# A transformer layer in fp32r parts on one Trainium2 core: whole blocks of the up product 512 columns wide, steps around the transposes and the down product's forms reordered, and the down weights of the second pass moved to another place modulo 256 bytes

## The chip, the cores and the metric

The kernel runs on one core of a Trainium2 chip. The metric is the time of one execution on the device in microseconds (us), taken several times, with the median as the figure to compare. One further execution is recorded by the hardware profiler; its timeline is called the trace here. The engines are named as the profile names them: PE (TensorE, matmuls) with PEld (its weight loads), DVE (VectorE), ACT (ScalarE), POOL (GpSimd) and SP (SyncE, which issues most of the DMAs).

## The reference

One layer over a sequence of 512 rows, width 1024, in float32:

```python
h  = _rmsnorm(x, g_pre_mix)
...
merged = jax.nn.sigmoid(a_ret) * y_ret + jax.nn.sigmoid(a_sgu) * y_sgu
x = x + _rmsnorm(merged @ w_out, g_post_mix)
h2 = _rmsnorm(x, g_pre_ffn)
x = x + _rmsnorm(_conv_gated_mlp(h2, w_up, conv_w, conv_b, w_down), g_post_ffn)
```

`y_ret` is a bidirectional retention (four heads, chunks of 128 rows), `y_sgu` a spatial gating unit. `_conv_gated_mlp` multiplies h2 by w_up (1024 x 5632, the *up product*), runs a depthwise convolution of three taps along the sequence, takes gelu of the first half times the second (2816 columns), and multiplies by w_down (2816 x 1024, the *down product*). `merged @ w_out` is called the *output product* below. The change touches the stretch from the output product to the end.

## The kernel before

**Parts.** A float32 product is made of three matmuls of fp32r operands. Each operand is split into a high and a low part (`split`, lines 85 to 87): ACT copies the high part (L80), DVE subtracts it from the source and so writes the low part (L87). `mm3` (lines 218 to 221, the matmuls' rows L219 to L221) issues high by high, high by low and low by high. In a matmul the first operand is the stationary one (128 x 128, loaded ahead by PEld), the second the moving one; the number of moving columns, 256 (*narrow*) or 512 (*wide*), is the matmul's length. Sums lie in PSUM banks of 512 columns; a bank is free again when DVE or ACT has read it.

**Weights.** They lie in DRAM as 146 units of 128 x 1024, in the order of use, and SP loads each by one DMA into one of 4 `raw` buffers. `w_get` hands out the next unit and makes the splits of up to four units ahead, so the splits' place on ACT and DVE follows the order of the program: what the program issues ahead of a `w_get` stands ahead of that unit's splits in their queues. The parts go to nine slots of 1088 floats (4352 bytes, 17 x 256). The second argument of `slot` (L124) is an offset in floats. In the built program a slot without an offset begins at 64 bytes modulo 256; with 16 floats it begins at 128, with 48 at 0. This *place* modulo 256 bytes is meant when the text says that a part lies at 0, 64 or 128. The other tiles of 512 floats (`blk`) begin at 64.

**Up product.** It has 44 blocks of 128 columns of w_up: 22 tiles in the gated half and as many in the other. Two kinds of steps make them. Tiles that are not in a couple are *whole blocks* (`up_block` L933, `h2_block` L927): weights stationary, the parts of h2 transposed (h2h, h2l) moving, first for the rows 0 to 255 (`T0`), then for 256 to 511 (`T1`), 24 narrow matmuls each. Sixteen tiles form eight couples: the two blocks of the first are made by a 2 x 2 scheme of the Strassen kind with seven products of 12 narrow matmuls instead of eight (`Pair`, L660, matmuls at L676), whose weight sums DVE and POOL make (L166 to L170, `wf` are their parts), and the two of the second are whole blocks, between the parts of the first. `c` tiles collect a Pair's results (L704 is one such reading of a bank). The output gate products earlier in the kernel (`gated_pair`) have the same scheme, with whole blocks that are 512 wide already (`f_block`, L646).

**Turns.** After the output product of a tile of 128 rows, `norms` (L858) makes x1 and scales it (L882); `turn` (L890) transposes it on PE, with ACT copying the high parts and raw copies, and DVE making the low parts (L901). Tiles 0 and 1 are turned during the output products of tiles 2 and 3. Then four blocks (`EARLY`) of the up product run on T0, with the turn of tile 2 behind the first of them and the turn of tile 3 behind the fourth, and then the same four on T1. `row_scale` takes a power on POOL (L849).

**Down product.** It has two passes, one for each half of the output columns. A pass has nine steps (`products`, L1050, matmuls at L1062), each with the seven products of the 2 x 2 scheme over a pair of gated tiles, 42 narrow matmuls, and four tiles outside the scheme (`add_whole`, L1068, matmuls at L1079). Here the activations are stationary and the weights (`q` and `t` units, parts dh and dl) move. A step's activation side is made by `down_forms` (L994): five DVE steps of 256 columns and three of 512, with their copies on ACT. Seven of the nine *forms* (`EAGER`) are made while the up product runs, the last two ahead of the second and the fourth step of the first pass, and the four tiles outside the scheme are split ahead of its first four steps. At the end of a pass DVE and ACT read the banks and add them up (`steps`; L1094 is the second sum of `after7`), which frees the banks for the second pass. Then rows are scaled, added to x1 and written.

Of the kernel before, what the change touches and what calls it, by code (L numbers as in the profile page):

```python
# [10 lines left out]
F32 = mybir.dt.float32  # L11
# [17 lines left out]
LOOK = 4  # L29
NBLK = 76  # L30
WARM = 18
# [3 lines left out]
WHOLE = NF - 2 * DP  # L35
EAGER = 7
ADDED = (0, 2)
# [11 lines left out]
def tile_block(ctx: ExitStack, tc, xT, x, wall, par, cs, wsp, bsp, gpost, gpre, gffn, out):  # L49
# [11 lines left out]
    def blk(dt=F32, n="blk", shape=(P, S)):  # L61
        return sb.tile(list(shape), dt, tag="blk", bufs=NBLK, name=nm(n))

    def tmp(n="tmp", shape=(P, S)):
        return sb.tile(list(shape), F32, tag="tmp", bufs=6, name=nm(n))
# [19 lines left out]
    def split(hi, lo, src):  # L85
        copy(hi, src)
        nc.vector.tensor_sub(lo, src, as32(hi))  # L87

# [7 lines left out]
    while i < NW:  # L96
# [19 lines left out]
        else:  # L116
            units.append(("blk", i))
            i += 1
    w_ready, w_pos, w_held, w_raw = {}, [0, 0], [0], {}

# [6 lines left out]
    def w_block(i):  # L127
# [48 lines left out]
    def w_down(form, i):  # L176
# [61 lines left out]

    xh, xl, xg = [], [], {}

    def load_x(k):
        t = tmp("xT")
        nc.sync.dma_start(t, xT[k])
        h_, l_ = blk(F32R, "xh"), blk(F32R, "xl")
# [598 lines left out]
    def row_scale(q):  # L843
# [9 lines left out]
    gpm, gpf = bcast(gpost, "gpm"), bcast(gpre, "gpr")  # L853
    h2h, h2l, h2r = ([[blk(dt, n) for _ in range(4)] for _ in range(2)]
                     for dt, n in ((F32R, "h2h"), (F32R, "h2l"), (F32, "h2r")))
    x1 = [[dp_.tile([P, S], F32, tag=f"x1_{t}{n}", name=f"x1_{t}{n}") for n in range(2)] for t in range(NT)]

    def norms(t, acc):  # L858
# [9 lines left out]
        for n in range(2):  # L868
            z = tmp("z")
            v.scalar_tensor_tensor(  # L870
                out=z, in0=acc[n], scalar=sc, in1=gpm[n], op0=ALU.mult, op1=ALU.mult
            )
            v.tensor_add(xt[n], xt[n], z)
            mean_square(q, n, xt[n])
            nc.gpsimd.dma_start(x1[t][n], xt[n])
            if n == 0 and t in ADDED:
                nc.gpsimd.dma_start(out[t, :, 0:S], xt[0])
        sc, _ = row_scale(q)
        zs = []
# [7 lines left out]

    two = "p (i n) -> p i n"

    def turn(t, zs):  # L890
        g, c = t // 2, slice((t % 2) * P, (t % 2 + 1) * P)
        for n in range(2):
            p = ps()
            for f in range(4):
                nc.tensor.transpose(p[:, f * P : (f + 1) * P], zs[n][:, f * P : (f + 1) * P], ident)
            for i in range(2):
                hi, lo, raw = (h[g][2 * n + i].rearrange(two, i=2)[:, :, c] for h in (h2h, h2l, h2r))
                pf = p[:, 2 * i * P : 2 * (i + 1) * P].rearrange(two, i=2)
                copy(hi, pf)
                copy(raw, pf)  # L900
                v.tensor_sub(lo, pf, as32(hi))  # L901

    def h2(k, t):
        f = slice((k % 2) * 256, (k % 2 + 1) * 256)
        g = t.start // 256
        return h2h[g][k // 2][:, f], h2l[g][k // 2][:, f]

# [18 lines left out]

    def h2_block(w, o, q):  # L927
# [12 lines left out]

    early_w, early_o = [], []

    def early(e, q):

        if q == 0:
            early_w.append(w_get(1))
            early_o.append(ps())
        h2_block(early_w[e], early_o[e], (T0, T1)[q])

    dn_ = Down(mh, ml, KD, RES_OUT)  # L950
    zs = {}
    for t in range(NT):
        acc = [dn_.finish(t, 0)]
        if t > 1:
            turn(t - 2, zs[t - 2])
        acc.append(dn_.finish(t, 1))
        zs[t] = norms(t, acc)
    early(0, 0)
    turn(2, zs[2])
    for e in range(1, EARLY):  # L960
        early(e, 0)
    turn(3, zs[3])
    for e in range(EARLY):
# [24 lines left out]

    def two_parts(t):
        h_, l_ = blk(F32R, "fh"), blk(F32R, "fl")  # L990
        split(h_, l_, t)
        return h_, l_

    def down_forms(j):  # L994
# [8 lines left out]
        v.tensor_add(a[:, T1], b[:, T0], s_[:, T1])  # L1003
        bh, bl = two_parts(b)
        sh, sl = two_parts(s_)
        th, tl = two_parts(a)
        dforms.append({
# [99 lines left out]
    for j in range(DP):  # L1107
        if j < WHOLE:
            whole.append(two_parts(gp[2 * DP + j]))
        if j % 2 and late:  # L1110
            down_forms(late.pop(0))
        products(m, j, steps if j == DP - 1 else {})
        if j in (3, 5):
            w = w_get()
# [209 lines left out]
```

## Time and profile before

| | |
|---|---|
| time, median of 3 runs | 829.57 us (828.09 to 830.15) |
| the profiled execution's own time | 826.92 us |
| its span | 825.1 us |
| PE busy | 814.5 us (99% of the span) |
| DVE, ACT, POOL busy | 658.5, 429.7, 104.2 us |
| output product, with the turns of tiles 0 and 1 | 426.3 to 471.6 us |
| four early blocks, with the turns of tiles 2 and 3 | 471.6 to 518.4 us |
| other blocks of the up product | 518.4 to 703.9 us |
| down product, first and second pass | 703.9 to 760.5, 760.5 to 816.4 us |

The stretches are read from the first matmul of each. "Busy" of PE counts a matmul from its start to a modelled end, and the ends of pipelined matmuls overlap; so the interval between the starts of two matmuls tells what one costs. The page names instructions by line, engine, operation, and `out<-in` with the program's tile names; a shape as 128x512 is partitions by elements. Where the profile names a releaser, it is the work on another engine whose end let the instruction start.

### The profile page before, as it was taken

What the parts mean: (1) busy time and instruction counts of PE and PEld (TensorE: products, weight loads), DVE (VectorE), ACT (ScalarE), POOL (GpSimd) and SP (SyncE); (2) the same over time, 40 slices, a digit from 0 to 9 for tenths busy, and PEclk for the clock granted to TensorE, in tenths of its full rate; (3) what the DMA queues carried; (4) which work ended last, traced back from release to release, by engine and by line L of the source; (5) the groups of instructions that cost most, each with busy time, mean ns of one, the idle gap of its engine ahead of it and who ended that gap; (6) DMA issues with size and microseconds to landing.
All of it is one profiled execution on the core that took longest, in us unless ns stands there. A gap on an engine that the chain in (4) does not pass through costs nothing. (4 is left out here: it accounts for less than half of the span.)

```text
span 825.1 us, 14353 instructions
## 1 busy us (share of the span) xinstructions
PE 814.5 (99%) x5728; PEld 756.6 (92%) x5728; DVE 658.5 (80%) x1076; ACT 429.7 (52%) x733; POOL 104.2 (13%) x108
## 2 busy tenths in 40 slices
PE   9999999999999999999999999999999999999995
PEld 7888888888999999999988899999999999999995
DVE  7489897878898687767765579679899899997956
ACT  6636445536665444444444556456566566644532
POOL 0010000103221111132221201111111100000002
PEclk9999999999999999999999999999999999999999
DMA  8733222213233333233459111333333341243334
GB/s 284 256 116 102 77 77 77 77 52 94 74 105 127 103 103 101 80 101 102 123 173 355 64 54 50 104 102 103 103 103 103 102 155 52 77 141 104 114 129 128
DMA packets 29252, 93.84 MB, mean 114 GB/s; under 512 B 3392, under 2 KB 4032, under 8 KB 29184
## 3 DMA queue, kind: packets, MB, share of 16 engines
q1 hardware_dynamic: 26784, 86.58, 32.5%
q0 software_dynamic: 1968, 6.03, 2.4%
q8 instruction: 45, 0.74, 0.4%
q10 hardware_dynamic: 432, 0.30, 0.1%
q14 instruction: 23, 0.19, 0.1%
HBM read 88.19 MB, written 4.72 MB: 113 GB/s over the span
## 5 line engine op out<-in xcount | busy, mean ns | idle before, releaser
L87 DVE TENSOR_TENSOR wl<-raw,wh 128x1024 fp32r<-128x1024 f32 (+1 forms) x93 | 109.6, 1187 | 49.2 <-PE ps L676 26.5
L80 ACT ACTIVATE wf<-raw 128x512 fp32r<-128x512 f32 x140 | 85.0, 626 | 102.4 <-PE ps L220 42.7
L87 DVE TENSOR_TENSOR wf<-raw,wf 128x512 fp32r<-128x512 f32 x140 | 110.1, 801 | 26.1 <-ACT wf L80 25.4
L220 PE MATMUL ps<-h2l,wh 128*128 128x256 f32 x448 | 123.7, 277 | 0.2 <-DVE h2l L901 0.2
L219 PE MATMUL ps<-h2h,wh 128*128 128x256 f32 x448 | 123.3, 277 | 0.0
L221 PE MATMUL ps<-h2h,wl 128*128 128x256 f32 x448 | 123.3, 276 | 0.0
L676 PE MATMUL ps<-sh,wf 128*128 128x256 f32 x640 | 119.1, 277 | 0.1
L80 ACT ACTIVATE wh<-raw 128x1024 fp32r<-128x1024 f32 (+2 forms) x95 | 93.0, 989 | 35.5 <-DMA raw<-wall 14.0
L676 PEld LDWEIGHTS ps<-sh,wf 128*128 128x128 f32 x640 | 100.7, 188 | 0.8 <-DVE c L704 0.3
L676 PE MATMUL ps<-sl,wf 128*128 128x256 f32 x320 | 88.5, 277 | 0.0
L220 PEld LDWEIGHTS ps<-h2l,wh 128*128 128x128 f32 x448 | 84.0, 188 | 0.7 <-DVE h2l L901 0.7
L219 PEld LDWEIGHTS ps<-h2h,wh 128*128 128x128 f32 x448 | 83.8, 188 | 0.3 <-ACT h2h L80 0.3
L221 PEld LDWEIGHTS ps<-h2h,wl 128*128 128x128 f32 x448 | 83.9, 188 | 0.0
L481 PE MATMUL ps<-wh,xh 128*128 128x512 f32 x192 | 75.0, 391 | 0.0
L482 PE MATMUL ps<-wl,xh 128*128 128x512 f32 x192 | 74.9, 390 | 0.0
L483 PE MATMUL ps<-wh,xl 128*128 128x512 f32 x192 | 74.8, 390 | 0.0
L168 POOL TENSOR_TENSOR raw<-raw,raw 128x512 f32<-128x512 f32 x20 | 34.9, 1743 | 241.0 <-DVE raw L166 217.0
L1062 PE MATMUL ps<-dh,fl 128*128 128x256 f32 x216 | 61.0, 282 | 0.0
L1062 PE MATMUL ps<-dl,fh 128*128 128x256 f32 x216 | 60.3, 279 | 0.5 <-DVE dl L87 0.5
L1062 PE MATMUL ps<-dh,fh 128*128 128x256 f32 x216 | 60.6, 280 | 0.0
L676 PEld LDWEIGHTS ps<-sl,wf 128*128 128x128 f32 x320 | 60.1, 188 | 0.5 <-issue 0.2
L676 PE MATMUL ps<-xh,wf 128*128 128x256 f32 x288 | 53.6, 278 | 0.0
(309 smaller groups left out, 2035.0 us busy)
## 6 DMA issues: line engine op xcount, KB each, us to landing
raw<-wall SPq DMA_DIRECT2D x145, 512.0 KB, 3.6
x<-x SPq DMA_DIRECT2D x22, 256.0 KB, 5.7
xT<-xT SPq DMA_DIRECT2D x8, 256.0 KB, 5.3
x<-x POOLq DMA_DIRECT2D x8, 256.0 KB, 2.4
xT<-xT POOLq DMA_DIRECT2D x4, 256.0 KB, 4.3
out<-zs SPq DMA_DIRECT2D x3, 256.0 KB, 3.4
cs<-cs SPq DMA_DIRECT2D x2, 256.0 KB, 4.0
gpm<-gpost POOLq DMA_DIRECT2D x2, 256.0 KB, 3.7
```

What stands on the lines that cost most here:

```text
L80: nc.scalar.activation(out=o, in_=i, func=AF.Copy)
L87: nc.vector.tensor_sub(lo, src, as32(hi))
L168: nc.gpsimd.tensor_tensor(out=w_raw["T2"], in0=w_raw["T1"], in1=w_raw["B22"], op=ALU.add)
L219: nc.tensor.matmul(o, ah, bh, start=start, stop=False)
L220: nc.tensor.matmul(o, ah, bl, start=False, stop=False)
L221: nc.tensor.matmul(o, al, bh, start=False, stop=stop)
L481: nc.tensor.matmul(acc[t], xh[k][:, c], wh[:, f], start=k == 0, stop=False)
L482: nc.tensor.matmul(acc[t], xh[k][:, c], wl[:, f], start=False, stop=False)
L483: nc.tensor.matmul(acc[t], xl[k][:, c], wh[:, f], start=False, stop=k == KD - 1)
L676: nc.tensor.matmul(o, w_[:, c], a_, start=first and k == n == 0, stop=k == 3 and n == 2, skip_group_check=True,)
L1062: nc.tensor.matmul(o, a_[:, c], w_[:, f], start=j == t == i == 0, stop=j == DP - 1 and i == 2 and n not in (M2, M3, M4), skip_group_check= ...
```

## The change

- **Width.** The whole blocks of the up product behind the four early ones, 24 of them, run all 512 rows in one matmul: 24 wide ones for each block instead of 48 narrow ones. So that a matmul can take 512 rows at once, h2h and h2l lie in tiles of twice the width (`two`), with all rows of one 128-wide piece of the width side by side. `Pair.part3`, which ran between the two halves of a block, now runs in its middle. Weight slots of these blocks have no offset any more. The early blocks stay in halves.
- **Turns.** In `turn` the high copies and the low parts come first, the raw copies last. The scaling is taken out of `norms` into `scaled`, and that of tile 2 is issued behind the low parts of the turn of tile 1. The turn of tile 3 comes in the middle of the fourth early block.
- **Late forms.** `EAGER` is 5 instead of 7. The four later forms and the four tiles outside the scheme are issued behind the steps of the first pass, from a list, and each group is placed behind the low part of the next step's `t` weights (`tc.issue_after`).
- **Places in the down product.** In the first pass both weight parts of a step keep their offsets; in the second both have 48, so all moving parts lie at 0 there; the stationary ones stay at 64.

```diff
-            hi, lo = (slot("wh", 16), slot("wl", 48)) if i >= DOWN0 else (
-                (slot("wh", 48), slot("wl", 16)) if i >= UP0 else (slot("wh"), slot("wl"))
+            hi, lo = (slot("wh", 48), slot("wl", 48)) if i >= DOWN0 + DP + WHOLE // 2 else (
+                (slot("wh", 16), slot("wl", 48)) if i >= DOWN0 else
+                (slot("wh", 48), slot("wl", 16)) if UP0 <= i < UP0 + EARLY else (slot("wh"), slot("wl"))
             )
...
-        hi, lo = slot("dh", 16, w), slot("dl", 48, w)
-        split(hi, lo, raw)
+        at = (16, 48) if i < DOWN0 + DP + WHOLE // 2 else (48, 48)
+        hi, lo = slot("dh", at[0], w), slot("dl", at[1], w)
+        w_low[form, i] = split(hi, lo, raw).ins
...
             for i in range(2):
-                hi, lo, raw = (h[g][2 * n + i].rearrange(two, i=2)[:, :, c] for h in (h2h, h2l, h2r))
...
                 copy(hi, pf)
-                copy(raw, pf)
-                v.tensor_sub(lo, pf, as32(hi))
+                low = v.tensor_sub(lo, pf, as32(hi))
+                raws.append((raw, pf))
+        for raw, pf in raws:
+            copy(raw, pf)
+        return low
...
     def up_block(between=None):
-        w, o = w_get(), ps()
-        h2_block(w, o, T0)
-        if between:
-            between()
-        h2_block(w, o, T1)
+        (wh, wl), o = w_get(), ps()
+        for k in range(KD):
+            if between and k == KD // 2:
+                between()
+            c = slice(k * P, (k + 1) * P)
+            mm3(o, wh[:, c], wl[:, c], *h2(k, slice(0, S)), k == 0, k == KD - 1)
         return o
...
         acc = [dn_.finish(t, 0)]
         if t > 1:
-            turn(t - 2, zs[t - 2])
+            low = turn(t - 2, zs[t - 2])
+        if t == 3:
+            with tc.issue_after(low.ins):
+                zs[2] = scaled(*xq)
         acc.append(dn_.finish(t, 1))
-        zs[t] = norms(t, acc)
+        xq = norms(t, acc)
+        if t != 2:
+            zs[t] = scaled(*xq)
     early(0, 0)
     turn(2, zs[2])
     for e in range(1, EARLY):
-        early(e, 0)
-    turn(3, zs[3])
+        early(e, 0, (lambda: turn(3, zs[3])) if e == EARLY - 1 else None)
...
-    late = list(range(EAGER, DP))
+    later = (("w", 0), ("w", 1), ("f", 5), ("w", 2), ("f", 6), ("w", 3), ("f", 7), ("f", 8))
...
     for j in range(DP):
-        if j < WHOLE:
-            whole.append(two_parts(gp[2 * DP + j]))
-        if j % 2 and late:
-            down_forms(late.pop(0))
         products(m, j, steps if j == DP - 1 else {})
+        if j + 1 < DP:
+            with tc.issue_after(w_low["t", DOWN0 + j + 1]):
+                for kind, i in {0: later[:1], 1: later[1:3], 2: later[3:4], 3: later[4:6], 4: later[6:7], 5: later[7:]}.get(j, ()):
...
```

The program has 5115 matmuls and transposes afterwards instead of 5691. Besides those rows on PE, the order moves at three places on DVE. Line numbers afterwards are a little higher for the same statement: L87 is L91, L901 is L911, L882 is L893, L704 is L712.

The first place is DVE during the output product of the last tile of rows, where the turn of tile 1 is read: `h2l` are the low parts of h2, `xn` the scaled tile 2, `x` its x1. Before:

```order
L873 TENSOR_TENSOR x_844_4735<-x_844_4735,z_4755 128x512
L846 SCALAR_TENSOR_TENSOR qs_4761<-q_4747 128x1
L882 SCALAR_TENSOR_TENSOR xn_4765<-x_843_4734,qr_4762,gpr_4379 128x512
L882 SCALAR_TENSOR_TENSOR xn_4767<-x_844_4735,qr_4762,gpr_4380 128x512
L901 TENSOR_TENSOR h2l_4391<-ps_4787,h2h_4383 128x2x128
L901 TENSOR_TENSOR h2l_4393<-ps_4798,h2h_4385 128x2x128
L901 TENSOR_TENSOR h2l_4392<-ps_4787,h2h_4384 128x2x128
L901 TENSOR_TENSOR h2l_4394<-ps_4798,h2h_4386 128x2x128
```

And now:

```order
L881 TENSOR_TENSOR x_828_4719<-x_828_4719,z_4739 128x512
L911 TENSOR_TENSOR h2l_4379<-ps_4763,h2h_4375 128x2x128
L911 TENSOR_TENSOR h2l_4380<-ps_4763,h2h_4376 128x2x128
L911 TENSOR_TENSOR h2l_4381<-ps_4772,h2h_4377 128x2x128
L911 TENSOR_TENSOR h2l_4382<-ps_4772,h2h_4378 128x2x128
L854 SCALAR_TENSOR_TENSOR qs_4785<-q_4731 128x1
L893 SCALAR_TENSOR_TENSOR xn_4789<-x_827_4718,qr_4786,gpr_4371 128x512
L893 SCALAR_TENSOR_TENSOR xn_4791<-x_828_4719,qr_4786,gpr_4372 128x512
```

The four low parts stand ahead of the two scaling steps (and the step in front of those) instead of behind them.

The second place is DVE in a couple of the up product, where a weight sum for the next couple is made: `raw` are the sums, `wf` their parts, `fl` a part of a form, `c` a Pair's result, whose reading frees a bank. Before:

```order
L87 TENSOR_TENSOR fl_6507<-gp_5314,fh_6506 128x512
L166 TENSOR_TENSOR raw_6585<-raw_6562 128x512
L167 TENSOR_TENSOR raw_6562<-raw_6562,raw_6563 128x512
L87 TENSOR_TENSOR wf_6589<-raw_6585,wf_6589 128x512
L704 TENSOR_TENSOR c_6511<-ps_6514,c_6511 128x256
L87 TENSOR_TENSOR wf_6641<-raw_6585,wf_6641 128x512
```

And now:

```order
L91 TENSOR_TENSOR fl_6203<-gp_5250,fh_6202 128x512
L171 TENSOR_TENSOR raw_6281<-raw_6258 128x512
L172 TENSOR_TENSOR raw_6258<-raw_6258,raw_6259 128x512
L712 TENSOR_TENSOR c_6207<-ps_6210,c_6207 128x256
L91 TENSOR_TENSOR wf_6285<-raw_6281,wf_6285 128x512
L91 TENSOR_TENSOR wf_6313<-raw_6281,wf_6313 128x512
```

The reading of the bank has moved ahead of the part `wf` that follows the two sums.

The third place is DVE in the first pass of the down product, up to the low part of the `t` weights (`dl` 128x1024) of its fourth step. Rows of one form are `fa`, `fs`, `fl` and the two sums into `gp`; before, the form here is the eighth:

```order
L87 TENSOR_TENSOR fl_7956<-gp_7571,fh_7955 128x512
L87 TENSOR_TENSOR fa_7959<-gp_7033,fa_7959 128x256
L1000 TENSOR_TENSOR fs_7962<-gp_7033,gp_7044 128x256
L185 TENSOR_TENSOR raw_8117<-raw_8063 128x512
L1001 TENSOR_TENSOR fs_7962<-fs_7962,gp_7033 128x256
L87 TENSOR_TENSOR fl_7968<-gp_7044,fh_7967 128x512
L1002 TENSOR_TENSOR gp_7033<-gp_7033 128x256
L87 TENSOR_TENSOR fl_7972<-fs_7962,fh_7971 128x512
L1003 TENSOR_TENSOR gp_7033<-gp_7044,fs_7962 128x256
L87 TENSOR_TENSOR dl_8008<-raw_8003,dh_8007 128x1024
```

And now it is the sixth:

```order
L91 TENSOR_TENSOR fl_7380<-gp_7075,fh_7379 128x512
L91 TENSOR_TENSOR dl_7326<-raw_7323,dh_7325 128x768
L91 TENSOR_TENSOR fa_7383<-gp_6173,fa_7383 128x256
L1023 TENSOR_TENSOR fs_7386<-gp_6173,gp_6184 128x256
L1024 TENSOR_TENSOR fs_7386<-fs_7386,gp_6173 128x256
L91 TENSOR_TENSOR fl_7392<-gp_6184,fh_7391 128x512
L91 TENSOR_TENSOR dl_7352<-raw_7347,dh_7351 128x1024
L1025 TENSOR_TENSOR gp_6173<-gp_6173 128x256
L91 TENSOR_TENSOR fl_7396<-fs_7386,fh_7395 128x512
```

The weight part (dl 128x1024) stands behind two steps fewer of the form, and the form here is one that the pass needs in its sixth step instead of its eighth.

More of the change, by code (lines that the diff above doesn't have):

```diff
@@ L35 @@
 WHOLE = NF - 2 * DP
-EAGER = 7
+EAGER = 5
+WIDE = 7
 ADDED = (0, 2)
@@ L62, in blk, with two @@
         return sb.tile(list(shape), dt, tag="blk", bufs=NBLK, name=nm(n))
+    def two(dt=F32R, n="two"):
+        return sb.tile([P, 2 * S], dt, tag="two", bufs=8, name=nm(n))
     def tmp(n="tmp", shape=(P, S)):
@@ L853, in tile_block @@
     gpm, gpf = bcast(gpost, "gpm"), bcast(gpre, "gpr")
-    h2h, h2l, h2r = ([[blk(dt, n) for _ in range(4)] for _ in range(2)]
-                     for dt, n in ((F32R, "h2h"), (F32R, "h2l"), (F32, "h2r")))
+    h2h, h2l = ([two(n=n).rearrange("p (i s) -> p i s", i=2) for _ in range(4)] for n in ("h2h", "h2l"))
+    h2r = [[blk(n="h2r") for _ in range(4)] for _ in range(2)]
     x1 = [[dp_.tile([P, S], F32, tag=f"x1_{t}{n}", name=f"x1_{t}{n}") for n in range(2)] for t in range(NT)]
@@ L886, in norms @@
         return zs
-    two = "p (i n) -> p i n"
     def turn(t, zs):
         g, c = t // 2, slice((t % 2) * P, (t % 2 + 1) * P)
+        raws = []
         for n in range(2):
@@ L896, in turn @@
             for i in range(2):
[L897 to L898 removed]
+                hi, lo = (h[2 * n + i][:, :, t * P : (t + 1) * P] for h in (h2h, h2l))
+                raw = h2r[g][2 * n + i].rearrange("p (i n) -> p i n", i=2)[:, :, c]
+                pf = p[:, 2 * i * P : 2 * (i + 1) * P].rearrange("p (i n) -> p i n", i=2)
                 copy(hi, pf)
[L900 to L901 removed]
+                low = v.tensor_sub(lo, pf, as32(hi))
[3 more added lines that the diff above has]
+        return low
     def h2(k, t):
[L904 to L906 removed]
+        return tuple(h[k // 2][:, k % 2, t] for h in (h2h, h2l))
     h2forms = {n: [None] * 4 for n in ("S1", "S2", "S3", "S4")}
@@ L987, in gated, with two_parts @@
         v.tensor_mul(gp[-1], ca, cb)
-    def two_parts(t):
-        h_, l_ = blk(F32R, "fh"), blk(F32R, "fl")
+    def two_parts(t, wide=False):
+        if wide:
+            w = two(n="fw")
+            h_, l_ = w[:, :S], w[:, S:]
+        else:
+            h_, l_ = blk(F32R, "fh"), blk(F32R, "fl")
         split(h_, l_, t)
```

32 lines of the change are left out of this document (21 added, 11 removed).

## The prediction

> **What bounds the kernel now.** I read the page first, then who waited for whom on TensorE, then busy times by stretch. The page's head, its busy shares and its line of the granted TensorE clock:
>
> ```profile
> span 825.1 us, 14353 instructions
> PE 814.5 (99%) x5728; PEld 756.6 (92%) x5728; DVE 658.5 (80%) x1076; ACT 429.7 (52%) x733; POOL 104.2 (13%) x108
> PEclk9999999999999999999999999999999999999999
> ```
>
> TensorE is busy from end to end at full clock. Its waits, in the answers on who waited for whom (engine, line, releaser: us in total, times, longest), are few and short:
>
> ```profile
> PE ps L1062 <- DVE dl L87: 0.5, 1, 0.5
> PE ps L220 <- DVE h2l L901: 0.2, 1, 0.2
> PEld ps L676 <- DVE c L704: 0.3, 1, 0.3
> PEld ps L1062 <- DVE c L1094: 0.2, 1, 0.2
> ```
>
> So the time is the number of matmuls by the interval between two starts, plus a few stalls. "Busy" can't give the interval, because the ends are modelled and overlap. I take stretches that begin at a matmul's start and end 0.01 us before another's start. Their rows read: stretch, length, PE busy and instructions, clock, DMA share, GB/s. The count holds those still in flight at the left edge: two matmuls of 256 columns (narrow), or one of 512 (wide).
>
> ```profile
> 426.31:457.58 31.27, 31.27 (x139) 1.00 0.71 261
> 679.38:703.85 24.47, 24.47 (x218) 1.00 0.15 46
> 87.23:90.46 3.23, 3.23 (x29) 1.00 0.37 63
> 770.00:800.00 30.00, 30.00 (x257) 1.00 0.46 143
> 249.13:260.53 11.40, 11.40 (x98) 1.00 0.43 141
> 364.81:385.30 20.49, 20.49 (x133) 1.00 0.35 105
> 538.84:559.23 20.39, 20.39 (x182) 1.00 0.34 106
> ```
>
> Row 1, wide, the output product: 31.28/138 = 226.7 ns. Row 2, narrow, the end of the up product: 24.48/216 = 113.3, half of it. Row 3, narrow, retention: 3.24/27 = 120.0. Row 4, narrow, the down product's second pass: 30.0/255 = 117.6. So narrow matmuls have several intervals at one clock. What tells these rows apart in the built program is where their parts lie modulo 256 bytes. Up product: moving parts (h2h, h2l) all at 64, stationary at 0 and 128. Retention: both at 64. Down: moving weights at 128 (dh) and 0 (dl), stationary at 64. Wide matmuls with both at 64 (row 1) pay nothing. Row 5 is narrow with the up product's places and yet 11.41/96 = 118.9: that is a second, slow rhythm, which ends at the next wide block. Rows 6 and 7 are one gated pair with wide blocks (84 narrow, 48 wide) and one couple of the up product (180 narrow); both are used below.
>
> **The change, part by part.**
>
> *Wide blocks (24 of them; 1152 narrow matmuls become 576 wide).* Two narrow at 113.3 are 226.6, one wide is 226.7: nothing is won in the stream. The Trainium skill ("TensorE: Matmul & The Clock Gate", Back-to-back issue gap) gives N/2.4 + 2.5 ns for a warm matmul, by which one wide would save 2.5 ns on two narrow; as an estimate from it that is 1.4 us over the 576. The two rows show 0.1 ns the other way, and the sum goes by them. Alternating costs something: row 6 has the very sequence that a couple has afterwards, with 84 + 2 x 48 = 180 narrow matmuls' worth, and takes 20.50 against 20.40. Eight couples: **+0.8 us**. Below nothing this can't go, since no wide row is under 226.7.
>
> *Turns.* Here are the whole early stretch of the up product, its first block, the turn's eight transposes, the next three blocks, and the rest:
>
> ```profile
> 471.62:518.43 46.81, 46.55 (x401) 1.00 0.17 57
> 471.62:475.11 3.49, 3.27 (x25) 1.00 0.02 5
> 475.12:475.91 0.79, 0.79 (x10) 1.00 0.00 0
> 475.92:484.54 8.62, 8.62 (x75) 1.00 0.16 61
> 485.62:518.43 32.81, 32.80 (x288) 1.00 0.19 64
> ```
>
> It has 384 narrow matmuls, 43.5 us at 113.3, and two turns of 0.80 with some 0.1 behind each: 45.3. It takes 46.8, so 1.5 are lost: 3.50 - 2.72 = 0.8 in the first block of 24, 8.63 - 72 x 0.1133 = 0.5 in the next three, the rest at the second turn. DVE and ACT at that place:
>
> ```profile
> 470.12 1.41 DVE L882 SCALAR_TENSOR_TENSOR xn<-x,qr,gpr 128x512 f32<-128x512 f32 x2 [0.74 <-POOL qr L849]
> 471.46 0.74 DVE L901 TENSOR_TENSOR h2l<-ps,h2h 128x256 fp32r<-128x256 f32 x2
> 472.60 0.98 DVE L901 TENSOR_TENSOR h2l<-ps,h2h 128x256 fp32r<-128x256 f32 x2 [0.39 <-ACT h2r L80]
> 467.64 0.36 ACT L80 ACTIVATE h2h<-ps 128x256 fp32r<-128x256 f32 x1
> 471.90 0.38 ACT L80 ACTIVATE h2h<-ps 128x256 fp32r<-128x256 f32 x1 [1.33 <-DVE h2l L901]
> 479.23 1.41 DVE L882 SCALAR_TENSOR_TENSOR xn<-x,qr,gpr 128x512 f32<-128x512 f32 x2 [0.75 <-POOL qr L849]
> ```
>
> The first high part is there at 468.0, its low part only at 471.46, since DVE scales two tiles first. ACT's next high part waits for that, while TensorE wants all four by 473.7. Afterwards the low parts come first on DVE, the raw copies last on ACT: four steps of about 0.8 us from 468.3 end near 471.5, and the 0.8 goes. Queued behind are the two scaling steps; their reader, the turn of tile 2, comes 2.7 us after 471.6, and 1.4 suffice. The last turn moves ahead of half a block (12 matmuls, 1.4 us), which covers its first parts; it then stands near 482, and its input, ready at 480.6 now, is ready sooner. Bounds 1.1 (the slow rhythm stays in the 84 matmuls ahead of it) to 1.5; I take **-1.3**.
>
> *A stall in a couple.* The stalled products, 24 clean ones, and DVE and POOL there:
>
> ```profile
> 635.40:638.57 3.17, 3.10 (x26) 1.00 0.00 0
> 638.58:641.29 2.71, 2.71 (x26) 1.00 0.13 15
> 635.04 1.66 DVE L87 TENSOR_TENSOR wf<-raw,wf 128x512 fp32r<-128x512 f32 x1
> 636.63 0.41 DVE L704 TENSOR_TENSOR c<-ps,c 128x256 f32<-128x256 f32 x1
> 634.51 1.65 POOL L168 TENSOR_TENSOR raw<-raw,raw 128x512 f32<-128x512 f32 x1 [16.78 <-DVE raw L166]
> ```
>
> DVE's wf takes 1.66 us beside a POOL instruction, and the c that frees the bank stands behind it. Afterwards c stands ahead: **-0.46**, or 0 if POOL holds another one.
>
> *Late forms.* Two products of the first pass, clean and stalled; DVE's late weight part; DVE over the pass; two groups of the forms' steps in it:
>
> ```profile
> 714.46:718.69 4.23, 4.23 (x38) 1.00 0.00 0
> 719.41:724.40 4.99, 4.51 (x38) 1.00 0.33 97
> 720.31 1.22 DVE L87 TENSOR_TENSOR dl<-raw,dh 128x1024 fp32r<-128x1024 f32 x1
> 703.86:760.45 56.59, 49.74 (x82) 1.00 0.33 107
> L87 DVE TENSOR_TENSOR fl<-gp,fh 128x512 fp32r<-128x512 f32 x11 | 7.5, 681 | 0.0
> L1001 DVE TENSOR_TENSOR fs<-fs,gp 128x256 f32<-128x256 f32 x3 | 1.2, 416 | 0.0
> ```
>
> The weight part of the fourth step comes late because form 7 stands ahead of it: 5.00 - 4.24 = 0.76. In the new order form 5 begins there, four steps ahead of that weight part, but forms 5 and 6 no longer fill DVE before the pass. A form is five steps of 0.42 and three of 0.68, 4.1 us. The pass held three, now it holds four; idle time falls from 6.85 to 2.7 us and stays above nothing. Form 8 has to be through by the last step of the pass, near 755. I take **-0.76**, bounds 0 and -0.76.
>
> *Pass two's places.* Moving parts now all lie at 0, stationary ones at 64. No row has this pair. The up product shares one place for all moving parts, off the stationary ones' (113.3); retention shares it with them (120.0). I take 113.3, being the nearer: 474 x 4.3 = 2.0. One wait eats 0.1 of it: the sixth product of the first step waits for DVE's c, and reaches it 30 x 4.3 ns sooner. **-1.9**, bounds -2.0 and 474 x 2.4 = +1.1. The DVE and ACT steps of this pass are as before.
>
> *The start.* ACT's order puts a scaling copy ahead of a weight copy:
>
> ```profile
> 6.27 0.63 ACT L80 ACTIVATE wh<-raw 128x512 fp32r<-128x512 f32 x1 [0.73 <-DMA raw<-wall]
> 11.39 0.71 ACT L257 ACTIVATE xg<-xT,part 128x512 f32<-128x512 f32 x1
> ```
>
> It fits into the 0.73 us in which ACT waits for that weight's DMA: 0, or 0.7 late if the DMA lands sooner.
>
> Sum: +0.8 - 1.3 - 0.46 - 0.76 - 1.9 = **-3.6**. It is made against the profiled execution, 826.92 us with a span of 825.1: 823.3. Against the median of the three runs, 829.57, it gives 826.0.
>
> **The rivals.** Runs can tell about 0.3% from nothing, 2.5 us: faster means below 827.1.
>
> *A: the place does nothing* in pass two, and it stays at 117.6. For it: the slow rhythm shows an interval that changes with the places kept. Against: 113.3, 117.6 and 120.0 go with the places elsewhere. -1.7: 827.9. The Trainium skill speaks for it (the same page, Part 2, step 1): TensorE reads moving and stationary operands by two ports of their own, so that loading weights takes nothing from the running matmul. This trace disagrees so far: three intervals at one width and clock.
>
> *B: pass two runs like retention*, at 120.0, since both its parts stand still. +1.1 instead of -1.9: 829.0.
>
> *C, slower: the slow rhythm takes the narrow products* between the wide blocks and stays. 672 of them in couples, 108 behind the last turn and 474 in pass two at 118.9 instead of 113.3: +7.0, so +3.4 and 833.0. It decides once about 1,100 of these 1,254 are caught (6.1 us). Against it: row 6, whose 84 narrow matmuls between wide blocks are not caught.
>
> **How the numbers follow.** Forecast 0.55, its own range 824.5 to 827.4 (the turns' and stalls' bounds; slow stretches like row 5's, 0.5 us, that come or not). A 0.22, B 0.10, C 0.08, 0.05 for waits that I don't see. Range: the best terms, with row 5's stretch gone and the runs' own spread, give 824.2; B with that spread 829.4. It leaves out C and tails. Faster: 0.45 of the forecast and 0.05 of A: 0.50. Slower: C, 0.03 unseen, 0.01 of B: 0.12. Same: 0.38.
>
> **What would show it.** Pass two at 113.3 a matmul from its second step; 20.5 us a couple; no wait for dl in pass one; the early stretch near 45.4; c ahead of wf and no wait for it. I am wrong where pass two stays at 117.6 (A), or where narrow stretches of the up product show 118.9 (C), or a late form stalls pass one's last steps.

## The result and the profile after

The changed kernel takes 824.55 us in the median of four runs (824.33 to 825.07), against 829.84 for the kernel before (four runs, 828.09 to 830.15). That is 5.3 us less where 3.6 were forecast. The ratio on record is 0.9945, 95% interval [0.9929, 0.9960]; the two medians alone give 0.9936. The profiled execution took 824.34 us against 826.92, which is only 2.6 us less. That the two differences differ is the first thing to explain. The head of the page after:

```profile
span 822.6 us, 13202 instructions
PE 811.8 (99%) x5152; PEld 732.1 (89%) x5152; DVE 658.4 (80%) x1076; ACT 431.1 (52%) x733; POOL 104.1 (13%) x108
PEclk9999999999999999999999999999999999999998
```

TensorE is still busy from end to end, at full clock but for the last slice. Its stages, each from the start of its first matmul to the start of the next stage, in us:

| stage | before | after | forecast | measured |
|---|---|---|---|---|
| up to the first early block | 471.62 | 471.46 | 0 | -0.16 |
| early stretch | 46.82 | 46.26 | -1.3 | -0.56 |
| couples and last tiles of the up product | 185.42 | 185.76 | +0.8 - 0.46 | +0.34 |
| pass one | 56.59 | 55.48 | -0.76 | -1.11 |
| pass two, to its last matmul | 55.95 | 55.05 | -1.9 | -0.90 |
| what is left of the span | 8.7 | 8.6 | 0 | -0.1 |

The early stretch holds, behind the four early blocks, the first four whole blocks too: 192 of its 384 narrow matmuls before, 96 wide ones after.

Stretches of the trace after, as in the prediction (length, PE busy and instructions in flight, clock, DMA share, GB/s): the first early block, the 60 narrow matmuls behind the turn of tile 2, the 108 behind the turn of tile 3, one couple, the last four and a half whole blocks, pass one, and a piece of pass two.

```profile
471.46:474.18 2.72, 2.72 (x25) 1.00 0.00 0
474.99:482.19 7.20, 7.20 (x63) 1.00 0.19 74
482.99:495.90 12.91, 12.91 (x111) 1.00 0.27 83
538.22:558.71 20.49, 20.49 (x133) 1.00 0.32 102
678.97:703.47 24.50, 24.50 (x110) 1.00 0.20 66
703.48:758.95 55.47, 55.47 (x475) 1.00 0.31 101
770.00:800.00 30.00, 30.00 (x267) 1.00 0.44 141
```

The first block takes 2.73 us instead of 3.50. The 168 narrow matmuls behind the turns take 7.21/60 = 120.2 and 12.92/108 = 119.6 ns: the slow rhythm. A couple takes 20.50, a wide matmul 24.51/108 = 226.9. Pass one has no wait left: 55.48/474 = 117.05, where it was 117.8 beside its wait. Pass two runs at 30.0/265 = 113.2. (A stretch with round ends gives the interval to within one matmul: read from start to start, 113.2 here and 117.6 below are 113.3 and 117.8.) Its first step waits longer than before, though; TensorE's waits and its weight loads' in this place:

```profile
PE ps L1085 <- DVE c L1117: 1.2, 1, 1.2
PEld ps L1085 <- DVE c L1117: 1.4, 1, 1.4
```

DVE's chain that ends in this `c`, by its first step (the sums of a `t` unit, which wait for the weights' DMA) and its last, of the kernel before:

```profile
757.71 0.69 DVE L185 TENSOR_TENSOR raw<-raw 128x512 f32<-128x512 f32 x1 [0.84 <-DMA raw<-wall]
763.39 0.68 DVE L1094 TENSOR_TENSOR c<-ps,uu 128x512 f32<-128x512 f32 x1
```

And after:

```profile
757.28 0.69 DVE L190 TENSOR_TENSOR raw<-raw 128x512 f32<-128x512 f32 x1 [1.49 <-DMA raw<-wall]
762.96 0.68 DVE L1117 TENSOR_TENSOR c<-ps,uu 128x512 f32<-128x512 f32 x1
```

From the start of the first to the end of the last, DVE works without a gap for 6.36 us in both kernels. The chain starts when the weights land, and this came only 0.43 us earlier, while pass one ended 1.49 us earlier. TensorE reaches the bank 1.6 us sooner and finds it free 0.43 sooner; the first step of pass two, 42 matmuls, takes 6.20 us instead of 4.76 (42 x 113.3), a loss of 1.45, where it took 5.20 instead of 4.95 before, a loss of 0.25.

### The profile page after: what moved, and what is told of

Its sections match the earlier page's. It is cut to its first block, busy times and chain, and to the rows that moved or that the text cites. A ratio compares the mean times of both kernels' runs of the same rounds, so it can differ in the third digit from the quotient of the medians.

```text
span 822.6 us, 13202 instructions
## 1 busy us (share of the span) xinstructions
PE 811.8 (99%) x5152; PEld 732.1 (89%) x5152; DVE 658.4 (80%) x1076; ACT 431.1 (52%) x733; POOL 104.1 (13%) x108
## 4 chain that ended last, share of the span: by engine, by line
PE 96%; DVE 1%; issue 1%; POOL 1%; DMA 0%; ACT 0%; POOLq 0%; DVEq 0%; ACTq 0%
PE ps L684 23%; PE ps L226 13%; PE ps L225 13%; PE ps L227 12%; PE ps L1085 10%; PE ps L489 5%; PE ps L490 5%; PE ps L491 5%; PE ps L838 2%; PE ps L839 2%; PE ps L840 2%; PE ps L1102 2%; PE ps L763 1%; PE ps L289 1%; PE ps L614 0%
## 5 line engine op out<-in xcount | busy, mean ns | idle before, releaser
L91 DVE TENSOR_TENSOR wl<-raw,wh 128x1024 fp32r<-128x1024 f32 (+1 forms) x93 | 109.3, 1184 | 48.6 <-PE ps L684 27.5
L91 DVE TENSOR_TENSOR wf<-raw,wf 128x512 fp32r<-128x512 f32 x140 | 110.8, 806 | 26.3 <-ACT wf L84 25.3
L684 PE MATMUL ps<-sh,wf 128*128 128x256 f32 x640 | 119.2, 277 | 0.0
L226 PE MATMUL ps<-h2l,wh 128*128 128x512 f32 (+1 forms) x256 | 93.1, 363 | 0.0
L225 PE MATMUL ps<-h2h,wh 128*128 128x512 f32 (+1 forms) x256 | 93.0, 363 | 0.0
L227 PE MATMUL ps<-h2h,wl 128*128 128x512 f32 (+1 forms) x256 | 92.5, 361 | 0.0
L227 PEld LDWEIGHTS ps<-h2h,wl 128*128 128x128 f32 x256 | 48.0, 188 | 7.7
L225 PEld LDWEIGHTS ps<-h2h,wh 128*128 128x128 f32 x256 | 48.1, 188 | 6.9
L226 PEld LDWEIGHTS ps<-h2l,wh 128*128 128x128 f32 x256 | 48.0, 188 | 6.6
L1085 PE MATMUL ps<-dh,fh 128*128 128x256 f32 x168 | 46.7, 278 | 1.2 <-DVE c L1117 1.2
L84 ACT ACTIVATE dh<-raw 128x768 fp32r<-128x768 f32 (+1 forms) x36 | 33.9, 948 | 24.8 <-PE ps L1085 17.9
L1085 PE MATMUL ps<-dl,fh 128*128 128x256 f32 x168 | 46.7, 278 | 0.0
```

Source lines behind the costliest of these rows:

```text
L84: nc.scalar.activation(out=o, in_=i, func=AF.Copy)
L91: return nc.vector.tensor_sub(lo, src, as32(hi))
L225: nc.tensor.matmul(o, ah, bh, start=start, stop=False)
L226: nc.tensor.matmul(o, ah, bl, start=False, stop=False)
L227: nc.tensor.matmul(o, al, bh, start=False, stop=stop)
L684: nc.tensor.matmul(o, w_[:, c], a_, start=first and k == n == 0, stop=k == 3 and n == 2, skip_group_check=True,)
```

## The experiments

The theory: the interval of a narrow matmul is a *rhythm* that TensorE keeps; the places of the parts decide which rhythms there are, and a wait or a wide matmul can change which one runs. The main rivals: the place does nothing, or it alone sets the interval. The changed kernel itself ran only beside the result. In the three sets of experiments the faster executions of the kernel before have medians of 826.7, 826.4 and 826.1 us, so a few tenths between a run below and the changed kernel's 824.55 say nothing.

**Pass two's place undone** (p2_old).

```diff
-            hi, lo = (slot("wh", 48), slot("wl", 48)) if i >= DOWN0 + DP + WHOLE // 2 else (
+            hi, lo = (slot("wh", 16), slot("wl", 48)) if i >= DOWN0 + DP + WHOLE // 2 else (
...
-        at = (16, 48) if i < DOWN0 + DP + WHOLE // 2 else (48, 48)
+        at = (16, 48)
```

> The changed kernel with the down weights of pass two back at 128 (high) and 0 (low). Theory (the place sets the interval): pass two goes back from 113.3 to about 117.3 ns a matmul, 474 x 4.0 = +1.9 us, less 0.1 since the wait in its first step gets shorter: 826.3 us. Rival (the place does nothing, pass two is faster for another reason): 113.3 stays and so does 824.5 us.

826.24 us (ratio 0.9977 [0.9966, 0.9989]). A piece of its pass two:

```profile
770.00:800.00 30.00, 30.00 (x257) 1.00 0.43 141
```

30.0/255 = 117.6 again, and 1.7 us more than the changed kernel: as the theory had it. That the place does nothing is refuted: its eleven runs (825.46 to 827.03) lie above all four of the changed kernel. Ahead of the wait in the first step the interval was 117.0 here and behind it 117.8, so the pair 128/0 and 64 has more than one interval as well:

```profile
758.65:761.80 3.15, 3.15 (x29) 1.00 0.40 95
```

That is 3.16/27 = 117.0.

**Pass one's weights at 0 as well** (p1_new).

```diff
-                (slot("wh", 16), slot("wl", 48)) if i >= DOWN0 else
+                (slot("wh", 48), slot("wl", 48)) if i >= DOWN0 else
...
-        at = (16, 48) if i < DOWN0 + DP + WHOLE // 2 else (48, 48)
+        at = (48, 48)
```

> The changed kernel with the weights of pass one at 0 as well. Theory (place, and DVE's chain at the end of pass one is held by the cycle of load and split): pass one runs at 113.3 instead of 117.05, 474 x 3.75 = 1.8 us less, but the wait in pass two's first step (1.34 us now) takes most of it back or a wait for weights comes in pass one: 823.0 to 824.5 us. Rival (place alone counts): 822.8 us with the wait as it is. Rival (place does nothing in pass one): 824.5 us, intervals at 117.

825.08 us (0.9959 [0.9945, 0.9973]). Pieces of its two passes:

```profile
710.00:720.00 10.00, 10.00 (x87) 1.00 0.32 109
770.00:800.00 30.00, 30.00 (x267) 1.00 0.43 142
```

Nothing is won. The time is nearest to the second rival's (the place does nothing in pass one, 824.5), and the theory's reason fails: pass one runs at 10.0/85 = 117.6 with the very pair of places at which pass two runs at 113.2, in one execution. So the place alone doesn't set the interval either. The pair 0 and 64 has two rhythms. The slow one goes on over the start of pass two, where the pair doesn't change here, up to the wait for `c`; behind the wait the fast one runs.

**A wait put ahead of pass one** (p1_gap): as p1_new, with one small step on DVE that TensorE waits for. It is issued behind `cv_first`, the first step of the last convolution.

```diff
...
+    late_in = dforms[0]["A11"][0][:, 0:1]
+    with tc.issue_after(cv_first[0].ins):
+        v.tensor_copy(late_in, as32(late_in))
     for j in range(DP):
```

> The kernel with pass one's weights at 0 too (825.1 us, pass one at 117.8) with one more step on DVE, a copy of 128 x 1 elements of the first stationary part onto itself, for which PE has to wait some 1 to 2 us at the start of pass one. Theory (a wait sets the rhythm): pass one at 113.3 behind it, 474 x 4.5 = -2.1, the added wait +1.5, and what DVE's chain takes back in pass two up to 1.5: 824.5 to 826 us. Rival (pass one has its interval from something else than the rhythm): 117.8 stays, +1.5, 826.6 us.

829.08 us (1.0013 [0.9996, 1.0030]). A piece of its pass one, and its waits in the two passes:

```profile
710.00:755.00 45.00, 45.00 (x400) 1.00 0.34 110
```

```profile
PE ps L1086 <- DVE c L1118: 2.3, 1, 2.3
PE ps L1086 <- DVE fa L1133: 2.0, 1, 2.0
```

45.0/398 = 113.1: with a wait ahead of it pass one takes the fast rhythm, as the theory said. The time is above what both said: the wait for `c` grew from 1.5 (p1_new) to 2.3 us, and with smaller waits around it the first two steps of pass two took 4.7 us more than their matmuls need. Pass one is 2.0 us shorter than in p1_new, and DVE's chain starts at its end instead of 1.2 us ahead of it: the last weights landed only 0.8 us sooner after the start of the pass.

**The whole blocks in halves again, their weights at 0 and 128** (narrow).

```diff
-                (slot("wh", 48), slot("wl", 16)) if UP0 <= i < UP0 + EARLY else (slot("wh"), slot("wl"))
+                (slot("wh", 48), slot("wl", 16)) if i >= UP0 else (slot("wh"), slot("wl"))
...
-        (wh, wl), o = w_get(), ps()
-        for k in range(KD):
...
-            mm3(o, wh[:, c], wl[:, c], *h2(k, slice(0, S)), k == 0, k == KD - 1)
+        w, o = w_get(), ps()
+        h2_block(w, o, T0)
+        if between:
+            between()
+        h2_block(w, o, T1)
```

> The changed kernel with the 24 whole blocks of the up product in halves of 256 again, their weight slots at 0 and 128 as before. Theory (slow rhythm comes and goes with narrow blocks): the clean execution wins 0.8 us in the couples, 823.7, but blocks caught in the slow rhythm cost 24 x 5.6 ns each half, up to 1152 x 5.6 = 6.5 us, so its times spread over 823.7 to 830 and its median lies 1 to 4 us above the changed kernel's. Rival (width is neutral but for the switches): 823.7 us with a spread of under 1 us.

832.79 us (1.0050 [1.0036, 1.0064]): slower than the kernel before, and above both expectations. Two stretches of its up product:

```profile
500.00:630.00 130.00, 130.00 (x1096) 1.00 0.30 97
640.00:700.00 60.00, 60.00 (x507) 1.00 0.33 104
```

130/1094 = 118.8 and 60/505 = 118.8. Every narrow matmul from the turn of tile 2 to the down product is in the slow rhythm, and its runs lie within 0.9 us of each other. The turns leave TensorE in the slow rhythm, and nothing behind them ends it; in the changed kernel the wide blocks do. Two more things differ in this trace, its pass one and the first step of its pass two:

```profile
712.42:768.24 55.82, 55.82 (x476) 1.00 0.31 101
768.25:773.02 4.77, 4.77 (x44) 1.00 0.46 151
```

Pass one is at 55.83/474 = 117.8 where the changed kernel has 117.05, and pass two loses nothing in its first step (4.78 for 42 matmuls). Against the changed kernel's trace the up product takes 9.3 us more, pass one 0.35 more and pass two 1.4 less. At the end of pass one DVE's order is another here, too: the sums for the weights, with which the chain above starts, stand behind the step that reads the first bank, not ahead of it.

**The same with the turn of tile 3 where it was** (narrow_turn3).

```diff
-        early(e, 0, (lambda: turn(3, zs[3])) if e == EARLY - 1 else None)
+        early(e, 0)
+    turn(3, zs[3])
```

> The narrow kernel of the first experiments (832.8 us, all its narrow matmuls at 118.9 from the third turn to the end of the up product) with the turn of tile 3 back behind the fourth early block, where the kernel before waits 0.3 us inside it. Theory (a rhythm is kept until a wait or a wide matmul; the wait in the third turn let the kernel before into the fast one): from 485 us on the intervals are 113.3, about 1855 matmuls x 5.6 ns = 10.4 us less: 822.5 us. Rival (the new tiles of h2h and h2l make narrow matmuls slow wherever they stand): 832.8 to 833.1 us.

825.75 us (0.9968 [0.9951, 0.9985]), in two groups: three runs at 822.7 to 822.9, nine at 825.4 to 826.7. The same two stretches, in an execution of 826.5 us:

```profile
500.00:630.00 130.00, 130.00 (x1149) 1.00 0.31 98
640.00:700.00 60.00, 60.00 (x507) 1.00 0.33 106
```

The first is at 130/1147 = 113.3, the second at 118.8. Between them lies the stall of the sixth couple, the wait for `c` (L704 in the prediction, L712 here); in this program `c` stands behind `wf` again. So the new tiles of h2h and h2l are not what is slow. The fast rhythm begins at the turn of tile 3, where TensorE waits, and ends at the later wait.

**The kernel before, two more traces** (before_again, before_3, no edit).

> The kernel before, unchanged, for a second trace. Theory (slow rhythm differs between executions): where its time is some us off 826.9, whole blocks of narrow matmuls stand at 118.9 instead of 113.3 in this trace, and they are others than in the first. Rival (all executions have the same intervals, the spread comes from elsewhere): the same stretches at 118.9 as before, and the difference lies in waits.

> The kernel before a third time, for the trace of one of its longer executions. Theory (the wait of 0.46 us in the sixth couple draws the rhythm): an execution of 829 us or more shows narrow matmuls at 118.9 from 637 us to the end of the up product at 704, 590 x 5.6 = 3.3 us more; one of 826 to 827 shows 113.3 there. Rival: an execution of 829 us or more with 113.3 in that stretch.

826.68 and 828.41 us. The stretch behind the sixth couple in the first trace of before, in before_again, and in before_3:

```profile
640.00:700.00 60.00, 60.00 (x531) 1.00 0.35 106
```

```profile
640.00:700.00 60.00, 60.00 (x532) 1.00 0.33 106
```

```profile
640.00:700.00 60.00, 60.00 (x507) 1.00 0.32 106
```

113.4, 113.2 and 118.8 ns. Both lack one slow stretch of the first trace, the one that ends at 260 us (0.7 us); before_3 has another, from the stall to the end of the up product: 587 matmuls in 69.8 us, where the other two traces take 66.55, 3.2 us less. Its pass one is shorter in return:

```profile
706.50:762.31 55.81, 55.81 (x476) 1.00 0.31 104
```

From start to start that is 55.83 instead of 56.59 us, without the wait for `dl`: behind the slower up product the fourth step's weights are there in time. Beside the experiments the kernel before ran 72 times, 33 of them at 825.3 to 827.6 and 39 at 828.2 to 830.2, and none between, so it has two times. That the slow stretch behind the stall is what parts them rests on three traces of it. The first trace was of the lower group, the median of the first runs of the upper.

**The place of pass two alone, on the kernel before** (b_place, the diff of p2_old the other way round).

> The kernel before with both weight parts of pass two at 0, and nothing else. Theory (a place pair that allows the fast rhythm): pass two at 113.3 behind its first wait, 474 x 4.3 = -2.0, the wait 0.13 longer: 1.9 us below the kernel before on the same chip, though single executions can draw 117.8 in pass two and gain nothing. Rival (the gain needs the other changes): pass two at 117.6 or 117.8, no gain.

827.07 us (0.9987 [0.9973, 1.0000]). Its up product behind the sixth couple, and its pass two:

```profile
640.00:700.00 60.00, 60.00 (x507) 1.00 0.32 106
770.00:800.00 30.00, 30.00 (x268) 1.00 0.44 149
```

Pass two is at 30.0/266 = 112.8, to within one matmul the fast interval, without the other changes. Eight of ten runs lie at 826.7 to 827.5; the one that was traced is among them and has the slow stretch ahead of pass two. Their median, 827.1, is 1.9 us below the upper group of the kernel before in the same set of runs (829.06 in the median). The fastest, 824.19, is 1.9 below the lower group's 826.13; the tenth, 825.70, fits neither. The interval of the ratio still touches 1, because the draw at the sixth couple is larger than the effect.

**The late forms alone, on the kernel before** (b_late: `EAGER` 5 and the list behind the steps).

> The kernel before with the late forms queued as in the changed kernel, and nothing else. Theory (DVE's chain at the end of pass one starts when the weight load lands, not when PE is through): the wait for dl goes and pass one is 0.76 us shorter, but the wait in pass two's first step grows from 0.25 to about 0.9: 0.1 us gained. Rival (the terms add up): 0.76 us gained, the wait in pass two as before.

826.47 us (0.9991 [0.9975, 1.0007]), with six runs at 825.8 to 826.6 and four at 829.4 to 829.9. Its pass one, and its wait in pass two:

```profile
703.47:759.29 55.82, 55.82 (x476) 1.00 0.30 100
```

```profile
PE ps L1062 <- DVE c L1094: 0.4, 1, 0.4
```

Pass one is 56.59 - 55.83 = 0.76 us shorter, exactly the forecast term. The first step of pass two loses 0.65 instead of 0.25: half of it goes again. The lower group's median is where the kernel before has it in the same set, 826.1. The upper group's (829.6) is not below the kernel before's (829.1) either, as before_3 leads one to expect: there the stall is absent anyway. The theory's 0.1 us is nearer here than the rival's 0.76.

**The turn of tile 3 back, in the changed kernel** (turn3_back, the diff of narrow_turn3 on the changed kernel).

> The changed kernel with the turn of tile 3 back behind the fourth early block alone. Theory: its wait of 0.3 us lets the 96 narrow matmuls behind it run at 113.3 instead of 119.7: -0.6 + 0.3, 824.3 us. Rival (the turn's place sets only its own wait): +0.3, 824.9 us, intervals at 119 until the next wide block.

824.83 us (0.9962 [0.9949, 0.9975]). The matmuls behind that turn, and pass two:

```profile
484.85:495.77 10.92, 10.92 (x93) 1.00 0.31 98
770.00:800.00 30.00, 30.00 (x257) 1.00 0.43 141
```

The theory's claim falls here: 92 matmuls in 10.93 us, 118.8 ns, although the turn waits as it does in narrow_turn3. And pass two is at 117.6 with both weights at 0. Ahead of its wait for `c` it was not:

```profile
758.58:761.63 3.05, 3.05 (x29) 1.00 0.44 129
```

3.06/27 = 113.3: the fast rhythm ran from the start of the pass and ended at the wait. In p1_new a wait in the same place led the other way. So a wait doesn't bring the fast rhythm; it may change it, to either side. The spread of this kernel, 824.1 to 827.1, would fit executions with and without the slow pass two (443 matmuls x 4.5 ns = 2.0 us); one trace doesn't show it.

**The wait in pass two made shorter** (free_early: one low part of weights, 1.22 us on DVE, behind the sums that free the bank).

```diff
-        w_low[form, i] = split(hi, lo, raw).ins
+        if (form, i) == ("t", DOWN0 + DP + WHOLE // 2 + 1):
+            copy(hi, raw)
+            w_low["held"] = lambda: nc.vector.tensor_sub(lo, raw, as32(hi))
+        else:
+            w_low[form, i] = split(hi, lo, raw).ins
...
-        v.tensor_sub(c12, m[M5], uu)
+        with tc.issue_after(v.tensor_sub(c12, m[M5], uu).ins):
+            w_low["held"]()
```

> The changed kernel with one low part of weights (1.22 us on DVE) moved behind the two sums that free the bank for which pass two waits 1.34 us in its first step. Theory (the place pair has two rhythms, and pass two is in the fast one from its first matmul, ahead of the wait): the wait shrinks by 1.2, pass two stays at 113.3: 823.4 us. Rival (it is the wait that sets the fast rhythm): pass two at 117.8, -1.2 + 2.1, 825.4 us.

823.72 us (0.9948 [0.9929, 0.9967]), pass two at 113.2. As the theory said, it is in the fast rhythm from its first matmuls, ahead of the wait. So it is in all seven traces whose weights move to 0 at the start of pass two, and in three of them (narrow, narrow_turn3, hybrid) there is no wait in the first step at all. The rival, that the wait sets it, falls. TensorE's wait, and the start of DVE's chain:

```profile
PE ps L1089 <- DVE c L1121: 0.8, 1, 0.8
```

```profile
758.34 0.69 DVE L190 TENSOR_TENSOR raw<-raw 128x512 f32<-128x512 f32 x1 [1.65 <-DMA raw<-wall]
```

The wait shrank from 1.2 to 0.8 us, by 0.4 and not by 1.2. Pass one ended at 759.34 here, so the chain began 1.0 us ahead of that end instead of 1.7: again the weights landed late. The time is the lowest median of all, 0.8 us below the changed kernel's, but runs of both overlap; that it is faster isn't shown.

**Narrow blocks with a wide one behind the stall** (hybrid: narrow_turn3 and free_early together, and from the sixth couple on the second block wide, its weights at 0 and 128 like those of the narrow ones).

> From the changed kernel: the earlier low part in front of pass two's wait (as in free_early), the turn of tile 3 back behind the fourth early block, and the whole blocks narrow again, but for the second block of each couple from the sixth on, which stays wide. Theory (a wait draws the rhythm anew, a wide block brings back the fast one): the wait in the sixth couple does no harm, since a wide block follows; all narrow matmuls from 486 us to the end of the up product at 113.3; 822.8 (the fast executions of narrow_turn3) less 0.8, plus 0.15 for the switches: 822.1 us, and 824 at most where the wait in pass two draws the slow rhythm. Rival (a wide block does not bring the fast rhythm back): two values, 822 and 825.3 us, as in narrow_turn3.

825.23 us (0.9960 [0.9946, 0.9974]), its runs within 0.7 us. Ahead of the stall, one wide half block behind it, and the last narrow blocks:

```profile
500.00:630.00 130.00, 130.00 (x1149) 1.00 0.30 99
652.98:655.77 2.79, 2.79 (x14) 1.00 0.00 0
682.72:700.00 17.28, 17.28 (x147) 1.00 0.10 33
```

The rival was right that a wide block does not bring the fast rhythm back: 12 wide matmuls take 2.80 us, 233 ns each instead of 227, and the narrow ones behind them stay at 17.28/145 = 119.2. The two values that it forecast did not come; there is one. The wide blocks of the changed kernel differ by their weights' place, 64 instead of 0 and 128, and these are followed by narrow ones at under 114 ns in every couple of all six traces that have them. They are also twice as many to a couple; no run parts the two.

## Why the prediction was right, and where its terms were off

The direction held, and the time fell into the range, 1.5 us below the 826.0 that the sum gave. The sum did not hold term by term: against the trace it promised 1.0 us too much, and 2.7 us came that were not in it. That one error made up for part of the other is luck.

- **Places in pass two, interval: right.** 113.3 was forecast from the up product's pair of places; p2_old and b_place show it alone. Rivals A and B fall. The argument was thin (the nearer of two rows), and what it didn't have is that this pair allows 117.6 too (p1_new, turn3_back).
- **Places in pass two, wait: the step that failed.** "One wait eats 0.1 of it" counted only what pass two itself gains ahead of the wait, and took DVE's chain to move along with pass one. The chain starts when weights land, and these came 0.43 us sooner while pass one ended 1.49 sooner. The wait cost 1.2 us more, not 0.1. In b_late it cost 0.4 with the late forms alone, in p1_gap it grew with a pass one at the fast interval. It is not the price of a short pass one as such: before_3 and b_place have the same 55.83 us as b_late and lose 0.2 us there, narrow and narrow_turn3 have it with the late forms and lose none, p1_new has it and loses 1.75. What fixes when the last weights land, DVE's order or the round of loads and splits, is open.
- **Late forms: right at their place**, -0.76 in b_late, and the last steps of the pass are not stalled. The other 0.35 of pass one's 1.11 is an interval of 117.05 instead of 117.8 at unchanged places. It goes with the width: pass one is at 117.05 in all four traces with these places that have wide matmuls right ahead of it (changed kernel, p2_old, turn3_back, free_early), and at 117.8 in all eight with narrow ones, narrow among them. Why is open. And the 0.76 is there only in executions of the kernel before whose up product is fast; before_3 has no such stall.
- **Turns: half.** The 0.8 in the first block came. The slow rhythm behind the turns did not go, but caught 168 matmuls instead of 72 (168 x 6.3 ns = 1.1 us): -0.56 instead of -1.3, outside the bounds given, which took the stay of the slow rhythm for the matmuls ahead of the turn only (84 by the prediction; there are 60, and the 108 behind the turn were caught too).
- **Width and the stall in the couple: right in the trace**, +0.34 as forecast. But +0.8 is not what the width is worth. The prediction noted that the slow rhythm ends at the next wide block, and used this for rival C alone. Read the other way it says that an up product without wide matmuls has nothing to end a slow rhythm, while the changed kernel has an end in each couple. In the kernel before a slow stretch of 3.2 us stood in one trace of three, and by the two groups of times in more than half of its executions; the trace that was costed had none. The groups are 2.9 us apart; 3.2 less the stall of 0.76 would be 2.4, and the rest has no account. With the turns of the changed kernel the narrow blocks cost 9.3 us in the up product and 8.2 in all (narrow, 832.79, against 824.55).
- **Rival C** came true in the early stretch only; in the couples the wide blocks keep it out.

So the sum of 3.6 was 1.0 too large for the trace (2.6). The median of before was of the upper group, and in all six traces with the changed kernel's couples no slow stretch stands there: that is the account of the rest, 2.7 us. Whether the changed kernel itself draws a slow pass two now and then, as turn3_back does, its four runs don't show.

## To carry to other kernels

Where the times of one kernel fall into two groups, find what differs between them before costing a change against one trace; a change that removes the draw was worth more in the median here than any of its terms. Terms that end at the same wait don't add: follow each saving to the next bank, buffer or weight load that is due at a fixed time. And a stretch of matmuls is best checked by its interval, start to start, since with PE at 99% the page shows a loss of 5% nowhere (113.3 against 118.8 ns here).

## What the runs showed of the hardware

- One pair of places, one width and one clock gave two steady intervals: 113.3 and 118.8 in the up product (moving parts at 64, stationary at 0 and 128), 113.2 and 117.6 in pass two (0 and 64). They last for over a thousand matmuls and change at a wait, at the transposes, at wide matmuls, or where the places change; a wait can change them to either side, in one program from execution to execution (before_again and before_3). Behind the transposes of tile 2 the slow one ran in all 14 traces. With the weights at 128 and 0 the two passes showed 117.05 and 117.8, the latter behind waits too, and never 113.3.
- Wide matmuls took 227 ns with both parts at 64 and 233 with the weights, there the stationary parts, at 0 and 128; behind the first narrow ones were fast, behind the second they stayed slow. The second kind stood among slow narrow ones only (hybrid).
- The Trainium skill ("TensorE: Matmul & The Clock Gate", Part 2, step 1) says that loading weights takes no read bandwidth from the running matmul, since they have ports of their own. The intervals here speak against it in one case: with the moving parts kept at 64, wide matmuls took 227 ns with the stationary ones at 64 and 233 with them at 0 and 128. That read bandwidth is the reason isn't shown. What in TensorE or the memory keeps a rhythm is open: in the records the next weight load starts 2 to 5 ns behind the matmul ahead of it in either.
